# Two plain pairs at the head of each feed-forward layer, and a mixer input part in another order

## The chip, the core and the metric

The program runs on one core of a Trainium2 chip. The metric is device time in microseconds from launch to end, median of three runs. The engines are TensorE (PE in the profile, its weight loads PEld), VectorE (DVE), ScalarE (ACT), GpSimd (POOL) and SyncE (SP), which here issues the DMAs.

## The reference, cut to what matters

Two layers of a hybrid encoder trunk, over 576 tokens (512 of a new stream and 64 of a running one), with model width 1024 and feed-forward width 2816. Everything is float32.

```python
def swiglu_half(x, g, w_gate, w_up, w_down):
    h = rmsnorm(x, g)
    return x + 0.5 * ((jax.nn.silu(h @ w_gate) * (h @ w_up)) @ w_down)

def layer(x, ...):
    x = swiglu_half(x, ffn1...)
    y, c_kv, k_r, wkv, shift = token_mixer(rmsnorm(x, lp['mix_norm']), ...)
    x = x + y
    x = mem_attend(x, mk, mv, lp)
    x = swiglu_half(x, ffn2...)

def token_mixer(h, ...):
    proj = h @ lp['w_in']
    c_q, c_kv, k_r, p_b = jnp.split(proj, ...)     # latents of the attention heads; p_b feeds the recurrence
    ...                                            # 8 attention heads from c_q, c_kv, k_r
    xs = p_b + lp['shift_mu'] * (prev - p_b)
    r, k, v, xw, xa, xg = jnp.split(xs, ...)
    ...                                            # per-token recurrence over r, decay, k, v, kk, a
    y = y + jnp.sum(r_h * k_h * lp['r_k'], -1, keepdims=True) * v_h     # the "bonus"
    out = jnp.concatenate([y_a, y_b], axis=-1) @ lp['w_out']
```

## The kernel before, in words

**Matmuls.** Activations lie transposed, 128 features by 576 tokens to a tile, `x[0]` to `x[7]`. A float32 operand is cut into a high and a low part (`split`, L241 to L248: ACT writes the high part, another engine subtracts it from the source for the low one), and a product takes three matmuls (`mm3`, L312 to L316: high by high, high by low, low by high). The 576 tokens go as two halves `hs` of 288.

**Feed-forward layer** (`ffn`, four in the program). `Norm` (L362) takes the eight tiles one by one: high part, low part, square, and the squares are added into `nacc`, five of the seven additions on POOL (L378). Its `rstd` comes later, from a matmul with ones, and is applied to what comes out of PSUM. The width 2816 is 22 columns of 128, taken in 11 pairs. Pair 0 is plain: `plain` multiplies by a 1024 x 128 column, 48 matmuls, once for gate and once for up, for two columns. The other ten pairs go by a Strassen-Winograd scheme with 7 products in place of 8 (`products`): each needs 28 right-hand tiles `s`, made once per layer from the normed `x` (`normed`, `winograd`: four sums on POOL for every two tiles, and seven splits, two of whose low parts POOL makes), and per pair sums and splits of weight blocks (`factors`, 14 splits and 8 sums for gate and up). The gated activations of pair 0 are put into tiles with the tag `xnh`/`xnl`, of which there are eight each, all holding the normed input that `plain` reads. Down-projections follow: for pair 0 by themselves, then for every two pairs (`outputs`), each group of matmuls evicted by DVE onto `x` (L485, L594).

**Mixer input part** (`mixer`, L603 to L842). `STEPS` names the order: `key`, `gate`, `norms`, `factors`, `inverse` and `rest` for four groups of heads, and `keys`, `queries`, `rotated`, `normed` for the latents. `factors` multiplies on POOL at L722 and L724, `rest` at L773, and POOL also makes the low part of half of each streamed weight (`by=(DVE, POOL)`, L659). `rest` stores `rv` (L774), makes the bonus with the matmuls of L779 and stores it. The two last `rest` come after all latents. `inverse` runs a chain of 15 short products and reductions, the products on POOL for groups 0 and 1, on DVE for 2 and 3. All that the recurrence needs is stored to DRAM, and `prepare` (L1012) loads it back chunk by chunk (`ck`, `bk`, `DI`, L1015 to L1018).

**What sets the order.** A scheduler at build time walks the code with a model of each engine and fixes one in-order stream per engine. A tile that reuses a buffer waits until the former owner has been read for the last time. Each engine then runs its stream in order, SP its DMA issues too.

Of the kernel before, what the change touches and what calls it, by code (L numbers as in the profile page):

```python
# [10 lines left out]
F32R = mybir.dt.float32r  # L11
# [39 lines left out]
for _n, _c in (("ones", 128), ("eps", 4), ("id", 128), ("bd", 128), ("cen", 128), ("sel8", 32), ("sel", 128), ("mA", 256), ("mD", 64),  # L51
# [7 lines left out]
NT = 13  # L59
AHEAD = 4  # L60

# [3 lines left out]
         ("inverse", 1), ("factors", 3), ("inverse", 2), ("rest", 1), ("inverse", 3), ("keys",), ("queries",), ("rotated",),  # L65
         ("normed",), ("rest", 2), ("rest", 3))
# [65 lines left out]
def build(tc, I, O):  # L132
# [179 lines left out]
    def mm3(out, w, a, first, last, **kw):  # L312
        (wh, wl), (ah, al) = w, a
        PE.matmul(out, wh, ah, start=first, stop=False, **kw)  # L314
        PE.matmul(out, wh, al, start=False, stop=False, **kw)  # L315
        PE.matmul(out, wl, ah, start=False, stop=last, **kw)  # L316
# [45 lines left out]
    class Norm:  # L362
        def __init__(self, tiles, gain, tag, psum=None):
            self.out, self.tag = [], psum
            n = len(tiles)
            acc = st([128, T], "nacc")
            for k, t in enumerate(tiles):
# [4 lines left out]
                if k == 0:  # L372
                    ACT.activation(out=acc, in_=t, func=AF.Square)
                else:
                    s = st([128, T], "nsq")
                    ACT.activation(out=s, in_=t, func=AF.Square)  # L376
# [24 lines left out]
    def ffn(l, which, V, aside=iter(()), final=None, given=()):  # L401
# [3 lines left out]
        sc = Scope("ffn", side[1], s=28, sh=2, sl=2, sraw=1, S=4, t=NT)  # L405
# [18 lines left out]
        def winograd(b11, b12, b21, b22, alloc):  # L424

            t3, t1, t2, t4 = (tmp() for _ in range(4))
            for o, a, b, op in ((t3, b22, b12, ALU.subtract), (t1, b12, b11, ALU.subtract), (t2, t3, b11, ALU.add), (t4, b21, t2, ALU.subtract)):
                POOL.tensor_tensor(out=o, in0=a, in1=b, op=op)
            out = {}
            for n, src in ((1, b11), (6, t2), (7, t3), (5, t1), (2, b21), (4, t4), (3, b22)):  # L430
                t = out[n] = alloc()
                split(src, (t[:, 0], t[:, 1]), None, POOL if n in (5, 2) else DVE)
            return out

        def normed(j):
            y = []
            for k in (2 * j, 2 * j + 1):
                t = st([128, T], turn("nsq", "nacc"))
                DVE.scalar_tensor_tensor(out=t, in0=x[k], scalar=V("n%d" % which, k), in1=nrm.rstd(), op0=ALU.mult, op1=ALU.mult)
                y.append(t)  # L440
            return winograd(*[t[:, s] for t in y for s in hs], lambda: st([128, 2, HT], "s", F32R))


        ws = Stream(*[wgu[l, f, i] for f in range(2) for i in range(2)][len(given):] + [wd[l, g] for g in range(2)], given=given)
        xs, acts = [], []

        def plain(act):
            w, out = ws.next, []
            for s in hs:
                p = ps1("b")[:, 0:HT]  # L450
                for k in range(8):
                    mm3(p, w[k], [t[:, s] for t in act[k]], k == 0, k == 7)
                out.append((s, p))
            ws.ahead()
            return out

        for f in range(2):
            pg = plain(nrm.out)
            r = nrm.rstd()
            pu = plain(nrm.out)  # L460
            gs = []
            for s, p in pg:
                g = tmp()
                DVE.tensor_tensor(out=g, in0=p, in1=r[:, s], op=ALU.mult)
                silu(out=g, in_=g, func=AF.Silu)
                gs.append(g)
            acts.append((st([128, T], "xnh", F32R), st([128, T], "xnl", F32R)))
            for (s, p), g in zip(pu, gs):
                u = tmp()
                DVE.tensor_tensor(out=u, in0=p, in1=r[:, s], op=ALU.mult)  # L470
                DVE.tensor_tensor(out=u, in0=u, in1=g, op=ALU.mult)
                split(u, [t[:, s] for t in acts[f]], None)
            xs += [normed(2 * f), normed(2 * f + 1)]
        for i in range(2):
            w = ws.next
            pd = [[ps1("b")[:, 0:HT] for s in hs] for m in range(4)]
            for f in range(2):
                for m in range(4):
                    for s, p in zip(hs, pd[m]):
                        mm3(p, w[2 * m + f], [t[:, s] for t in acts[f]], f == 0, f == 1)  # L480
            ws.ahead()
            for m in range(4):
                for s, p in zip(hs, pd[m]):
                    o = x[4 * i + m][:, s]
                    DVE.scalar_tensor_tensor(out=o, in0=p, scalar=0.5, in1=o, op0=ALU.mult, op1=ALU.add)  # L485
# [3 lines left out]
        for p in range(1, NF // 2):  # L489
            order += [[wgu[l, 2 * q + r, i] for r in range(2)] for q, i in [(1, 0)] * (p == 1) + [(p, 1)] + [(p + 1, 0)] * (p + 1 < NF // 2)]  # L490
            if p % 2 == 0:
                order += [[wds[l, p // 2 - 1, m]] for m in range(4)]
# [92 lines left out]
        def outputs(ms, acts, halfway=None):  # L585
            ws = [take() for m in ms]
            for a in [hs[0:1], hs[1:2]] if halfway else [hs]:
# [7 lines left out]
                if halfway and a == hs[0:1]:  # L595
                    halfway()
# [902 lines left out]
```

## Time and profile before

| | us |
|---|---|
| three runs | 2869.1, 2871.0, 2876.91 |
| median | 2871.0 |
| the profiled execution, its own time | 2865.1 |
| its span, first to last instruction | 2863.2 |

The profiled execution is 5.9 us below the median. In the rows further down, columns are these. A row of a stretch gives for each engine its busy time and, in brackets, the number of instructions, then the mean granted clock of TensorE (1.00 is its full 2.4 GHz, 0.50 the lower level of 1.2 GHz). A row in order of time gives start and duration in us, engine, line, operation, the tile written and those read, and in square brackets the idle time before it with what ended it. Since matmuls overlap in the engine, the number of them that start in a stretch says more than their busy time.

### The profile page before, as it was taken

The page shows a single profiled execution, that of the slowest core. Times are in us where ns is not written, and L with a number is a line of the kernel's source. Part 1 is how long each engine was busy: PE and PEld are TensorE (multiplying, and loading weights), DVE is VectorE, ACT ScalarE, POOL GpSimd, SP SyncE. Part 2 cuts the span into 40 slices and gives each one's busy share as a digit, 9 for nine tenths or more (in the row PEclk, how much of TensorE's full clock was granted, in tenths as well). Part 3 has the DMA queues.
Part 4 walks back from the last instruction along what each step waited for, and adds up shares of the span by engine and source line. Part 5 has one row for each costly group of instructions (what it writes and reads, how often), then busy time and mean ns, then how long its engine had stood idle before and what let it go on. Part 6 is the DMA issues. An engine that isn't in the chain of part 4 may idle for free.

```text
span 2863.2 us, 56005 instructions
## 1 busy us (share of the span) xinstructions
PE 2753.5 (96%) x22188; PEld 2641.8 (92%) x22188; DVE 2129.2 (74%) x4216; ACT 1368.5 (48%) x2813; POOL 383.1 (13%) x461
## 2 busy tenths in 40 slices
PE   6999999889999989999989999998999999899998
PEld 6999999878889889999989999997888899899998
DVE  8887775866666678777787777768666765887776
ACT  5544455345554544444444444553555445444444
POOL 5000013610000030000040000245010001300000
PEclk8999999989999999999999999999999999999999
DMA  4333333652333122222212222346433332122221
GB/s 171 111 126 108 104 115 94 151 157 84 94 121 122 63 82 89 93 92 89 82 60 97 96 89 89 126 111 141 140 94 121 99 115 71 67 89 96 90 95 64
DMA packets 187576, 293.22 MB, mean 102 GB/s; under 512 B 87066, under 2 KB 113050, under 8 KB 187138
## 3 DMA queue, kind: packets, MB, share of 16 engines
q1 hardware_dynamic: 185010, 285.46, 31.9%
q0 software_dynamic: 2304, 4.20, 0.6%
q8 instruction: 174, 2.85, 0.4%
q14 instruction: 88, 0.72, 0.1%
HBM read 250.36 MB, written 41.63 MB: 102 GB/s over the span
## 4 chain that ended last, share of the span: by engine, by line
PE 89%; DVE 6%; ACT 1%; issue 1%; DMA 1%; POOL 0%; SPq 0%; DVEq 0%; ACTq 0%; POOLq 0%
PE b L314 18%; PE b L316 18%; PE b L315 18%; PE mm L314 4%; PE mm L315 3%; PE g L314 3%; PE mm L316 3%; PE g L315 3%; PE g L316 3%; PE sm L1001 2%; PE pp L1001 2%; PE sc L314 2%; PE pp L1025 1%; PE sc L316 1%; PE sc L315 1%
## 5 line engine op out<-in xcount | busy, mean ns | idle before, releaser
L246 ACT ACTIVATE whi<-wraw 128x512 fp32r<-128x512 f32 (+1 forms) x520 | 321.4, 623 | 483.5 <-PE b L315 221.4
L316 PE MATMUL b<-s,wlo 128*128 128x288 f32 x1536 | 450.4, 295 | 0.0
L315 PE MATMUL b<-s,whi 128*128 128x288 f32 x1536 | 449.0, 293 | 0.0
L314 PE MATMUL b<-s,whi 128*128 128x288 f32 x1536 | 448.1, 295 | 0.0
L247 DVE TENSOR_TENSOR wlo<-wraw,whi 128x512 fp32r<-128x512 f32 (+1 forms) x484 | 344.3, 715 | 113.2 <-ACT whi L246 94.1
L314 PE MATMUL b<-xnh,whi 128*128 128x288 f32 x1152 | 344.5, 308 | 38.0 <-ACT xnh L246 16.2
L315 PE MATMUL b<-xnl,whi 128*128 128x288 f32 x1152 | 349.5, 305 | 13.2 <-DVE xnl L247 9.3
L316 PE MATMUL b<-xnh,wlo 128*128 128x288 f32 x1152 | 345.9, 302 | 0.0
L315 PEld LDWEIGHTS b<-s,whi 128*128 128x128 f32 x1536 | 288.7, 188 | 0.0
L316 PEld LDWEIGHTS b<-s,wlo 128*128 128x128 f32 x1536 | 288.3, 188 | 0.0
L314 PEld LDWEIGHTS b<-s,whi 128*128 128x128 f32 x1536 | 286.8, 188 | 0.0
L314 PEld LDWEIGHTS b<-xnh,whi 128*128 128x128 f32 x1152 | 221.6, 196 | 44.6 <-ACT xnh L246 18.0
L378 POOL TENSOR_TENSOR nacc<-nacc,nsq 128x576 f32<-128x576 f32 x40 | 63.8, 1595 | 1399.6 <-ACT nsq L376 831.8
L594 DVE SCALAR_TENSOR_TENSOR x<-b,x 128x288 f32<-128x288 f32 x320 | 144.3, 455 | 140.7 <-PE b L316 140.4
L315 PEld LDWEIGHTS b<-xnl,whi 128*128 128x128 f32 x1152 | 225.4, 196 | 16.8 <-DVE xnl L247 11.3
L316 PEld LDWEIGHTS b<-xnh,wlo 128*128 128x128 f32 x1152 | 224.9, 196 | 0.1
L315 PE MATMUL b<-s,sh 128*128 128x288 f32 x704 | 208.7, 296 | 0.0
L314 PE MATMUL b<-s,sh 128*128 128x288 f32 x704 | 207.8, 295 | 0.0
L316 PE MATMUL b<-s,sl 128*128 128x288 f32 x704 | 207.8, 295 | 0.0
L246 ACT ACTIVATE whi<-S 128x512 fp32r<-128x512 f32 x188 | 118.0, 630 | 185.0 <-PE b L315 182.0
L314 PE MATMUL mm<-xnh,whi 128*128 128x288 f32 x688 | 205.1, 299 | 1.0 <-ACT xnh L370 1.0
L316 PE MATMUL mm<-xnh,wlo 128*128 128x288 f32 x688 | 203.6, 296 | 0.0
(455 smaller groups left out, 7517.3 us busy)
## 6 DMA issues: line engine op xcount, KB each, us to landing
wraw<-in_wgu SPq DMA_DIRECT2D x136, 512.0 KB
wraw<-in_wds SPq DMA_DIRECT2D x60, 512.0 KB
sraw<-in_wgu SPq DMA_DIRECT2D x40, 512.0 KB
wraw<-in_win SPq DMA_DIRECT2D x36, 512.0 KB
sraw<-in_wds SPq DMA_DIRECT2D x20, 512.0 KB
wraw<-in_wmk SPq DMA_DIRECT2D x16, 512.0 KB
wraw<-in_wmv SPq DMA_DIRECT2D x16, 512.0 KB
wraw<-in_wout SPq DMA_DIRECT2D x32, 256.0 KB
```

The source lines that it names most:

```text
L246: ACT.activation(out=h, in_=src, func=AF.Copy)
L247: by.tensor_tensor(out=lo, in0=src, in1=h.bitcast(F32), op=ALU.subtract)
L314: PE.matmul(out, wh, ah, start=first, stop=False, **kw)
L315: PE.matmul(out, wh, al, start=False, stop=False, **kw)
L316: PE.matmul(out, wl, ah, start=False, stop=last, **kw)
L378: e.tensor_tensor(out=acc, in0=acc, in1=s, op=ALU.add)
L594: DVE.scalar_tensor_tensor(out=o, in0=p, scalar=0.5, in1=o, op0=ALU.mult, op1=ALU.add)
L1001: PE.matmul(o, *f(p4, e), start=(n == 0 and p4 == 0), stop=(n == len(terms) - 1), skip_group_check=True)
L1025: PE.matmul(p[:, p4], bk[half(e), p4], ck[half(e), p4, 0:128], start=True, stop=True)
```

## The change

**Feed-forward.** `PLAIN = 2`: pairs 0 and 1 are plain (four columns), nine pairs go by the 7-product scheme. Plain weights come in half columns (`take(2)`), and `plain` runs both token halves over a half column before it goes on. The gated activations of the plain columns lie in `s`, `rr`, `a` and `rs` tiles. `right` makes the right-hand tiles of two `x` tiles after each plain column, wholly with DVE and ACT. The down-projection of pair 0 is put around the columns of pair 1, and that of pair 1 behind the first gate of pair 2. Pairs 2 to 9 are projected two by two, and pair 10 alone at the end. There are 9 `t` buffers for 13.

**Norm.** All squares come after the splits in the code, and all their sums are on DVE.

**Mixer.** L722, L724, L773 and the second weight half go from POOL to DVE. `rest` is cut into `rest` and `bonus`, the `rest` steps come before the latents, and the latents are last. The first chunk's products in `prepare` are ordered behind the first query matmuls (`after`).

```diff
-NT = 13
+NT = 9
+PLAIN = 2
-         ("inverse", 1), ("factors", 3), ("inverse", 2), ("rest", 1), ("inverse", 3), ("keys",), ("queries",), ("rotated",),
-         ("normed",), ("rest", 2), ("rest", 3))
+         ("inverse", 1), ("bonus", 0), ("factors", 3), ("inverse", 2), ("rest", 1), ("inverse", 3), ("rest", 2), ("bonus", 1),
+         ("rest", 3), ("bonus", 2), ("keys",), ("bonus", 3), ("queries",), ("rotated",), ("normed",))
...
-                    e = DVE if k in (6, 7) else POOL
-                    e.tensor_tensor(out=acc, in0=acc, in1=s, op=ALU.add)
+            acc = st([128, T], "nacc")
+            for k, t in enumerate(tiles):
+                s = st([128, T], "nsq") if k else acc
+                ACT.activation(out=s, in_=t, func=AF.Square)
+                if k:
+                    DVE.tensor_tensor(out=acc, in0=acc, in1=s, op=ALU.add)
...
-                POOL.tensor_tensor(out=o, in0=a, in1=b, op=op)
+                DVE.tensor_tensor(out=o, in0=a, in1=b, op=op)
-                split(src, (t[:, 0], t[:, 1]), None, POOL if n in (5, 2) else DVE)
+                split(src, (t[:, 0], t[:, 1]), None)
...
-            acts.append((st([128, T], "xnh", F32R), st([128, T], "xnl", F32R)))
+            act = [st([128, T], tag or turn("rr", "a", "rs"), F32R) for _ in range(2)]
...
+        for f in range(2 * PLAIN):
+            g = plain_gate()
+            if f == 3:
+                y = normed(f)
+            if f > 1:
+                all_outputs(acts[0:2], range(4 * f - 8, 4 * f - 4))
+            acts.append(plain_up(g, "s" if f < 2 else None))
+            xs.append(right(y if f == 3 else normed(f)))
+        g = gate()
+        all_outputs(acts[2:4])
+        acts = []
+        for p in pairs:
...
+            if (p - PLAIN) % 2:
+                all_outputs(acts)
+                acts = []
...
-        ws = Stream(*[win[l, j] for op in STEPS for j in columns(*op)], by=(DVE, POOL))
+        ws = Stream(*[win[l, j] for op in STEPS for j in columns(*op)])
-            POOL.tensor_tensor(out=kk, in0=kk, in1=av, op=ALU.mult)
+            DVE.tensor_tensor(out=kk, in0=kk, in1=av, op=ALU.mult)
-            POOL.tensor_tensor(out=xk, in0=xk, in1=av, op=ALU.mult)
+            DVE.tensor_tensor(out=xk, in0=xk, in1=av, op=ALU.mult)
-            POOL.tensor_tensor(out=rv[:, :, 0:64], in0=chunks(xr), in1=chunks(wts[p4]), op=ALU.mult)
+            DVE.tensor_tensor(out=rv[:, :, 0:64], in0=chunks(xr), in1=chunks(wts[p4]), op=ALU.mult)
...
+                    if c == order[0]:
+                        after(i, queried[0])
```

**Where instructions stand now.** VectorE in the second feed-forward layer of layer 0, before: `L471` ends the gated activation of the first plain column (`t`), and the row `xnl<-t,xnh` makes its low part.

```order
L471 TENSOR_TENSOR t<-t 128x288
L439 SCALAR_TENSOR_TENSOR nsq<-x,narrow,rstd 128x576
L247 TENSOR_TENSOR s<-t,s 128x288 x3
L247 TENSOR_TENSOR s<-nsq,s 128x288
L247 TENSOR_TENSOR s<-nacc,s 128x288
L247 TENSOR_TENSOR wlo<-wraw,whi 128x512
...
L464 TENSOR_TENSOR t<-b,rstd 128x288 x2
L247 TENSOR_TENSOR s<-t,s 128x288 x2
L470 TENSOR_TENSOR t<-b,rstd 128x288
L247 TENSOR_TENSOR s<-t,s 128x288
L247 TENSOR_TENSOR s<-nsq,s 128x288 x2
L247 TENSOR_TENSOR xnl<-t,xnh 128x288 x2
```

The same engine and layer in the changed kernel, at the third plain column: `L554` ends its gated activation and `a<-t,rr` makes the low part, in tiles of their own; `L501` are the sums that POOL made.

```order
L553 TENSOR_TENSOR t<-b,rstd 128x288 x2
L501 TENSOR_TENSOR t<-nacc,nsq 128x288
L501 TENSOR_TENSOR t<-nsq 128x288
L554 TENSOR_TENSOR t<-t 128x288
L248 TENSOR_TENSOR wlo<-wraw,whi 128x512
L554 TENSOR_TENSOR t<-t 128x288
L501 TENSOR_TENSOR t<-t,nsq 128x288
L248 TENSOR_TENSOR a<-t,rr 128x288
L501 TENSOR_TENSOR t<-nacc,t 128x288
L492 SCALAR_TENSOR_TENSOR nsq<-x,narrow,rstd 128x576
L248 TENSOR_TENSOR wlo<-wraw,whi 128x512
L248 TENSOR_TENSOR a<-t,rr 128x288
```

The activation's low part stands two to four rows behind its product instead of fourteen, and DVE has the sums in its own stream.

SyncE at the end of the mixer's input part in layer 0, before: the last `rest` stores `big` (L774), and the loads of the first chunk (`ck`, L1015) come three rows later. `d<-x` are the results of `inverse`, `d<-ad` the bonus.

```order
L766 DMA d_65<-x 36x16x16 x4
L256 DMA wraw<-in_wmv 128x1024
L842 DMA out_shift<-narrow 128x28
L766 DMA d_65<-x 36x16x16 x4
L774 DMA d_5259<-big 128x9x128
L782 DMA d_7068<-ad 128x576
L256 DMA wraw<-in_wmv 128x1024
L1015 DMA ck<-d_5259 128x768
L1016 DMA bk<-d_5260 128x512
L1018 DMA DI<-d_65 64x8x64 x2
```

SyncE at the same place in the changed kernel: the last `big` (L798), the bonus and two stores of latents (L846, L858), the loads of `ck` (L1043) and `bk`, and then the last results of `inverse` (L788), with the load of `DI` (L1046) behind them.

```order
L798 DMA d_5267<-big 128x9x128
L846 DMA out_ckv<-lx 128x576
L257 DMA wraw<-in_wmv 128x1024
L858 DMA out_krope<-lx 32x576
L810 DMA d_6919<-ad 128x576
L1043 DMA ck<-d_5267 128x768
...
L788 DMA d_65<-x 36x16x16 x4
L257 DMA wraw<-in_wmv 128x1024
L788 DMA d_65<-x 36x16x16 x4
L1046 DMA DI<-d_65 64x8x64 x4
```

Between the last store of `big` and the first load stands work of the latents; the last `inverse` is now what the first `DI` waits for.

## Rows read from the trace of the kernel before

**Rows 1.** The page, busy time, share of the span and instructions of each engine.
```profile
PE 2753.5 (96%) x22188; PEld 2641.8 (92%) x22188; DVE 2129.2 (74%) x4216; ACT 1368.5 (48%) x2813; POOL 383.1 (13%) x461
```
**Rows 2.** Busy time by stretch: starts of the four feed-forward layers, one steady stretch.
```profile
core 0: us, PE busy (x) PEld busy (x) DVE busy (x) ACT busy (x) POOL busy (x), PEclk, DMA share, GB/s
24.00:76.00 52.00, 40.67 (x243) 38.55 (x244) 47.97 (x81) 25.08 (x58) 29.02 (x24) 0.80 0.24 79
1036.00:1088.00 52.00, 41.16 (x261) 38.82 (x260) 47.82 (x80) 24.36 (x57) 25.64 (x24) 0.87 0.18 61
1444.00:1496.00 52.00, 42.97 (x283) 40.78 (x282) 49.14 (x85) 25.72 (x60) 27.39 (x24) 0.90 0.19 61
2448.00:2500.00 52.00, 43.88 (x278) 41.86 (x277) 48.50 (x84) 25.20 (x59) 27.29 (x24) 0.87 0.18 61
1100.00:1152.00 52.00, 52.00 (x395) 52.00 (x394) 44.67 (x87) 26.86 (x52) 0.00 (x0) 1.00 0.34 112
```
**Rows 3.** The same view of parts of the second start.
```profile
1030.60:1041.70 11.10, 10.62 (x77) 10.44 (x78) 5.38 (x11) 6.39 (x12) 0.00 (x0) 1.00 0.32 113
1057.70:1085.70 28.00, 17.16 (x84) 15.23 (x84) 27.36 (x50) 10.68 (x26) 13.14 (x13) 0.76 0.17 56
```
**Rows 4.** VectorE in order of time there: POOL silent at first, busy at the last row.
```profile
1041.69 0.82 DVE L464 TENSOR_TENSOR t<-b,rstd 128x288 f32<-128x288 f32 x2
1042.43 0.45 DVE L470 TENSOR_TENSOR t<-b,rstd 128x288 f32<-128x288 f32 x1
1042.79 1.54 DVE L439 SCALAR_TENSOR_TENSOR nsq<-x,narrow,rstd 128x576 f32<-128x576 f32 x2
1044.24 0.82 DVE L439 SCALAR_TENSOR_TENSOR nacc<-x,narrow,rstd 128x576 f32<-128x576 f32 x1
...
1045.34 0.69 DVE L247 TENSOR_TENSOR wlo<-wraw,whi 128x512 fp32r<-128x512 f32 x1
1045.94 0.46 DVE L247 TENSOR_TENSOR s<-nsq,s 128x288 fp32r<-128x288 f32 x1
...
1050.71 3.03 DVE L247 TENSOR_TENSOR s<-t,s 128x288 fp32r<-128x288 f32 x3
```
**Rows 5.** In order of time there, DVE, ACT and PE: the first activation tile.
```profile
1047.55 1.06 DVE L471 TENSOR_TENSOR t<-t 128x288 f32<-128x288 f32 x1
...
1058.60 0.76 ACT L246 ACTIVATE xnh<-t 128x288 fp32r<-128x288 f32 x2
...
1059.08 1.00 PE L314 MATMUL b<-xnh,whi 128*128 128x288 f32 x4 [1.36 <-ACT xnh L246]
```
**Rows 6.** Busy time by stretch: mixer input of layer 0 with its sum, sum of layer 1's.
```profile
538.00:558.00 20.00, 12.44 (x109) 10.47 (x108) 14.90 (x24) 7.53 (x12) 11.98 (x13) 0.83 0.79 173
...
578.00:598.00 20.00, 12.96 (x70) 10.81 (x68) 15.80 (x34) 10.07 (x21) 7.98 (x11) 0.82 0.69 175
598.00:614.00 16.00, 13.70 (x71) 12.98 (x72) 7.98 (x18) 6.55 (x14) 0.40 (x1) 0.69 0.68 166
sum 136.00, PE 118.18 PEld 107.25 DVE 104.96 ACT 55.02 POOL 68.20; mean PE 16.88 PEld 15.32 DVE 14.99 ACT 7.86 POOL 9.74
...
sum 130.00, PE 115.30 PEld 104.18 DVE 104.08 ACT 53.66 POOL 70.12; mean PE 16.47 PEld 14.88 DVE 14.87 ACT 7.67 POOL 10.02
```
**Rows 7.** The chain that ended last, between the last bonus and the recurrence: start, duration, what.
```profile
586.74 0.74 DVE xs L775
...
591.63 5.70 DMA d<-big
...
597.75 5.55 DMA bk<-d
603.34 1.16 PE pp L1025 x8
```
**Rows 8.** Lines by themselves, ns min/median/max; the last, of groups, busy us, mean ns.
```profile
L775 DVE SCALAR_TENSOR_TENSOR xs<-xs,narrow,xk x8: 801/806/3582, 502.0 to 2001.9; 128x576 f32<-128x576 f32 x8
L722 POOL TENSOR_TENSOR kk<-kk,x x8: 1416/1423/1942, 482.3 to 1952.4; 128x576 f32<-128x576 f32 x8
L247 POOL TENSOR_TENSOR wlo<-wraw,whi 128x512 fp32r<-128x512 f32 x36 | 48.3, 1341 | 53.0 <-ACT whi L246 53.0
```

More of the change, by code (lines that the diff above doesn't have):

```diff
@@ L315, in mm3 @@
         PE.matmul(out, wh, al, start=False, stop=False, **kw)
-        PE.matmul(out, wl, ah, start=False, stop=last, **kw)
+        return PE.matmul(out, wl, ah, start=False, stop=last, **kw)
     def mmT(p, w, act, first, last):
@@ L435, in normed @@
[L435 to L466, printed above, removed]
-            acts.append((st([128, T], "xnh", F32R), st([128, T], "xnl", F32R)))
[L468 to L485, printed above, removed]
@@ L494, in factors @@
+        order += [[wd[l, PLAIN, g]] for g in range(2)]
         def factors():
-            for aps in order:
+            for n, aps in enumerate(order):
+                if n < len(given):
+                    yield from given[n].parts
+                    continue
                 blocks = []
@@ L529, in ffn, with take @@
         made, ready = factors(), []
-        def take():
-            while len(ready) <= AHEAD:
+        def take(ahead=None):
+            while len(ready) <= (AHEAD if ahead is None else ahead):
                 hl = next(made, None)
@@ new lines, in outputs @@
+        def outputs(acts, ms, halfway=None):
+            n = len(acts)
+            per = 4 // n
+            ws = [take() for _ in range(len(ms) // per)]
+            for a in [hs[0:1], hs[1:2]] if halfway else [hs]:
+                for i, m in enumerate(ms):
+                    for s in a:
+                        p = ps1("b")[:, 0:HT]
+                        for f in range(n):
+                            mm3(p, cols(ws[i // per], i % per * n + f), [t[:, s] for t in acts[f]], f == 0, f == n - 1)
+                        o = x[m][:, s]
+                        DVE.scalar_tensor_tensor(out=o, in0=p, scalar=0.5, in1=o, op0=ALU.mult, op1=ALU.add)
+                if halfway and a == hs[0:1]:
+                    halfway()
@@ new lines, in all_outputs, with plain @@
+        def all_outputs(acts, ms=range(8)):
+            per = 4 // len(acts)
+            for m in ms[::per]:
+                outputs(acts, range(m, m + per))
+        def plain(act):
+            ps = [ps1("b")[:, 0:HT] for _ in hs]
+            for i in range(2):
+                w = take(2)
+                for s, p in zip(hs, ps):
+                    for k in range(4):
+                        mm3(p, cols(w, k), [t[:, s] for t in act[4 * i + k]], i + k == 0, i * k == 3)
+            return list(zip(hs, ps))
@@ L547, in products @@
                 for n in range(4):
[L548 removed]
+                    mm3(bank[at], cols(w, n), [bs[n][i][:, e] for e in range(2)], at == i and n == 0, n == 3, skip_group_check=True)
                 yield i, bank[at]
@@ L806, in mixer @@
         SP.dma_start(gD, xg)
-        at = {"key": key, "gate": gate, "norms": key_norms, "factors": factors, "inverse": inverse, "rest": rest}
+        at = {"key": key, "gate": gate, "norms": key_norms, "factors": factors, "inverse": inverse, "rest": rest, "bonus": bonus}
         for op, *n in STEPS:
```

114 lines of the change are left out of this document (64 added, 50 removed).

## Prediction

> **What bounds the kernel now.** I read the page's busy line first [rows 1]: TensorE is busy for 96% of the span, VectorE for 74%. So the time can only fall where TensorE is short of work, and the next view, busy time by stretch, is for finding those places. The steady stretch starts 395 matmuls in 52 us, 0.1316 us each [rows 2]. The heads of the four feed-forward layers start 243, 261, 283 and 278: 152 + 134 + 112 + 117 = 515 too few, or 515 x 0.1316 = 67.8 us. The reader should see that VectorE is busy there for about 48 of 52 us (0.92), and that the granted clock falls below 1.00 after TensorE has gone idle. In 28 us of the second head 84 matmuls start where 213 would fit, at clock 0.76 [rows 3].
>
> The rows in order of time say what TensorE waits for. The gated product was made at 1047.55, but its high part only starts at 1058.60, and the matmul that follows the tile's split comes at 1059.08 [rows 5]: 11 us lie between, since the split writes into a tile that the plain matmuls still read. After that VectorE, which makes the right-hand tiles, is itself late. Part of its lateness is length: while POOL is silent a 288-wide operation takes 0.37 us from start to start, a 576-wide one 0.73 and a 512-wide one 0.60; beside POOL's sums three 288-wide ones took 3.03, about 1.0 each [rows 4].
>
> In the mixer input part TensorE is idle for 136 - 118.2 = 17.8 us in layer 0 and 130 - 115.3 = 14.7 in layer 1 [rows 6]. In three stretches of layer 0 the clock was 0.83, 0.82 and 0.69, which is 6.8 + 7.2 + 9.9 = 23.9 us at the lower level, worth at most half, 12 us. The chain of waits tells the end of it: the last bonus product, a store of 5.70 us, a load of 5.55 us, and the recurrence's first matmul at 603.34, 16.6 us after the bonus [rows 7].
>
> **Plain pairs: added matmuls.** A pair by 7 products takes 168 matmuls for gate and up, a plain one 192. That is 24 more in each of four layers: 96 x 0.1316 = **+12.6 us**.
>
> **Plain pairs: the head's stall.** In the new order each activation has tiles that nobody reads at that time, so its low part stands right behind the product, and the 11 us wait goes. What is late next? TensorE now has 384 plain matmuls, 96 of projections and 12 of the first right-hand product before it needs the second product's tile, and 77 of these start before `rstd` arrives at 1041.7 [rows 3]. The other 415 last 415 x 0.1316 = 54.6 us. VectorE's stream has between the same points 89 operations of 288, 8 of 576 and 23 of 512: 89 x 0.37 + 8 x 0.73 + 23 x 0.60 = 52.6 us at the paces of [rows 4], or 57 at its 0.92 share. So it comes about 2.6 us late by the end, and is hardly ahead anywhere. I keep **4 us** of stall in each layer, **+16**, against the 17 that each loses now. The bounds are 0 (VectorE without gaps, 52.6 under 54.6) and 9 (half of today's loss). POOL's work hidden there is zero after the change: its 16 sums and 8 low parts in each layer have gone into the 89. The half-column weights move the same bytes, at a DMA share of about 0.2 [rows 2], and cost nothing. Nine `t` buffers: the most held at once are seven; if they ran out, VectorE would wait as it now does on the activation tile, which is the last rival.
>
> **Feed-forward ends.** With pair 10 alone, each output needs the newest activation. From its last product that is a VectorE sum and product (2 x 0.37), a high part on ACT (two took 0.76 [rows 5], so 0.38) and a low part (0.37): 1.5 us, nothing else queued for TensorE. Four times makes **+6**. The bounds: 0 if the memory or mixer weights' matmuls fill it, 4 each if VectorE's evictions (16 x 0.37 beside 8 x 0.73 of the next norm's low parts) are late.
>
> **Norm sums.** Five of 0.73 us go from POOL to VectorE in each of eight norms. I take nothing: the first 77 matmuls of a head run while `rstd` is made, at full pace [rows 3], and the sums replace POOL's in that shadow. Without that cover it is 5 x 0.73 = 3.7 us a norm; the range holds that for a few of them.
>
> **Mixer input part.** VectorE takes over 12 products of 576 (12 x 0.73 = 8.8 us) and 12 weight low parts in this stretch (12 x 0.60 = 7.2; the other six lie ahead of it): +16 us. POOL's own durations for these are 1.42 and 1.34 us [rows 8], some 33 us gone from POOL. What does that give back to VectorE? Its `xs` step took 3582 ns once, beside a median of 806 [rows 8]. Bounds: nothing, or 33 us times VectorE's busy share of 105/136, 25 us. I take 10, below the middle, because the median is close to the uncontended 0.73. VectorE then needs 105 + 16 - 10 = 111 us, at a share of 0.92 121 of the 136 us; in layer 1 104 + 16 - 10 = 110, or 120 of 130.
>
> TensorE's side: with the stores first, the 5.70 and 5.55 us transfers lie beside the latents. What is late next is the latents' own chain into the first query, behind which the first chunk's products are now ordered, with the whole recurrence queued after them. It isn't shown before; bounds 0 and the 16.6 us of the chain that it replaces [rows 7], I take half, 8. SyncE passes the last `inverse` stores late, and the loads of `DI` queue behind; a store and a load of that kind are within the same 16.6. So TensorE needs 118.2 - 12 + 8 = 114. The larger of 121 and 114 binds in layer 0 (gain 15), 120 in layer 1 (gain 10): **-25**. Bounds: a loss of 50 (below), and a gain of 17.8 + 12 + 14.7 + 12 = 56 if all idleness and slow clock goes.
>
> **The sum.** The profiled execution took 2865.1 us. 2865.1 - 67.8 + 16 + 12.6 + 6 - 25 = 2806.9. It lies 5.9 below the median of the runs, 2871.0, so the forecast for the median is 2806.9 + 5.9 = **2813 us**. A change within 0.3% (8.6 us) cannot be told from none.
>
> **Rivals.** *VectorE binds the mixers.* If nothing comes back from POOL's silence, 121/0.92 = 132 of 136 and 120/0.92 = 130 of 130: no gain there worth counting. 2806.9 + 25 + 5.9 = 2838. For it: the median of 806, which leaves little to return. Against it: the one step of 3582 [rows 8], on the kind of operation that the last chain starts from [rows 7].
>
> *POOL's silence gives everything back.* VectorE's long operations vanish, heads need 52.6 us under a cover of 54.6 (no stall), and the mixers' VectorE needs 105 + 16 - 25 = 96, at its 0.92 share 104 us, so TensorE binds, with 114 of 136 and 115.3 - 12 + 8 = 111 of 130: gains of 22 and 19 in place of 15 and 10. 2806.9 - 16 - 16 + 5.9 = 2781. For it: 1.0 against 0.37 [rows 4]. Against it: the median 806 [rows 8]. The Trainium skill (SBUF — State Buffer, "Who interferes with whom") says that a VectorE instruction with two SBUF inputs and a GpSimd one that reads SBUF contend, and describes the contested port pair as an exclusive lock. By that rule each microsecond of POOL's reading costs VectorE up to the same, the side of this rival; the 3582 ns agree with it for one instruction, the median does not show it for the rest.
>
> *VectorE only gets more work* (the slower side). The long operations are then the stage's own and not POOL's doing. If a quarter of the 89 in each head still take 1.0 us, their mean is 0.53 and VectorE needs 89 x 0.53 + 5.8 + 13.8 = 66.8 us, 12 more than the cover (48 in place of 16); in the mixers 105 + 19 = 124 at today's share of 0.77 need 161 for 136, 25 more in each layer. 2865.1 - 67.8 + 48 + 12.6 + 6 + 50 + 5.9 = 2920. It decides from the point where VectorE's mean 576-wide two-input operation stays above 0.9 us with POOL silent. Against it: the rows in which POOL is silent hold 0.37 and 0.73 at the same tiles [rows 4]. The Trainium skill (Perfetto Trace Analysis, "Optimizing Scalar/DVE Operations") advises the reverse of this change: where VectorE is saturated, work may go to other engines, even GpSimd, though the two share a port and it might not help. VectorE at 0.92 in the heads is the case that the advice means; by it alone the 48 and 50 of this rival would stand.
>
> *The change doesn't remove the wait.* The new activation tiles or the nine `t` still have readers when the split wants them, about 12 us stay in each head, and the mixers gain nothing: 2865.1 - 67.8 + 48 + 12.6 + 6 + 5.9 = 2870, no change.
>
> **How the numbers follow.** Chances: the forecast 0.58, with a range of its own of 2787 to 2834 (its stall terms at 0 or 7 us a layer, the mixers at 10 either way); VectorE binding the mixers 0.17; everything given back 0.14; VectorE with only more work 0.06; the wait stays 0.05. The range for 8 in 10 leaves out the last two and the outer parts of the second and third, some 0.2 together: from 2774 to 2850. Faster by over 0.3% are the first three, 0.89; within 0.3% the wait that stays, 0.05; slower, with VectorE's extra work, 0.06.
>
> **What would show it.** Heads: 350 or more matmuls in those 52 us stretches at clock 1.00, and no wait of TensorE on an activation tile; 288-wide low parts at 0.37 us beside the sums. If the stall stays, the row of `a<-t` or the `s` low part that TensorE waits for names the engine. Ends: 1 to 2 us of idle TensorE before the first output of pair 10. Mixers: VectorE's busy share near 0.9 and no idle TensorE before a load of `bk`; in its place a wait on the latents' norm, or on `DI`. No `xs` step near 3.6 us. I would be wrong if VectorE's 576-wide operations stayed above 0.9 us, if the heads waited on weights instead, or if the recurrence's start moved later by more than the 16.6 us that it has now.

## The result, and the profile after

| | before | changed kernel |
|---|---|---|
| median, us | 2870.05 | 2836.54 |
| lowest to highest of four runs, us | 2865.87 to 2876.91 | 2832.89 to 2839.47 |
| the profiled execution, us | 2865.1 | 2836.0 |
| its span, us | 2863.2 | 2834.2 |

The ratio is 0.9884, with a 95% interval of 0.9866 to 0.9903. The kernel became 33.5 us faster where 58 were forecast; 2836.5 lies in the range of 2774 to 2850.

The page's busy line, which answers [rows 1]:

```profile
PE 2745.4 (97%) x22284; PEld 2634.1 (93%) x22284; DVE 2116.6 (75%) x4412; ACT 1351.2 (48%) x2781; POOL 136.2 (5%) x265
```

POOL has lost 196 instructions and 247 us. VectorE has 196 instructions more and yet is busy 12.6 us less. So its instructions have become shorter, as the forecast supposed: in the second head three 288-wide low parts take 1.19 us together in order of time, where they took 3.03 [rows 4]:

```profile
1041.13 1.19 DVE L248 TENSOR_TENSOR s<-t,s 128x288 fp32r<-128x288 f32 x3
```

The heads of the four feed-forward layers by stretch, which answer [rows 2]:

```profile
24.00:76.00 52.00, 52.00 (x395) 52.00 (x394) 48.83 (x113) 25.08 (x57) 0.00 (x0) 1.00 0.29 97
1026.00:1078.00 52.00, 52.00 (x392) 51.79 (x391) 46.35 (x105) 26.11 (x59) 0.00 (x0) 1.00 0.23 75
1424.00:1476.00 52.00, 50.35 (x364) 49.79 (x365) 45.91 (x103) 25.60 (x59) 0.00 (x0) 0.97 0.21 72
2429.00:2481.00 52.00, 52.00 (x391) 51.79 (x390) 46.35 (x105) 26.10 (x59) 0.00 (x0) 1.00 0.23 76
```

Where 243 to 283 matmuls started, 364 to 395 do, with the clock at 1.00 in three of the four. The third stretch begins while TensorE still waits for the norm sums of the layer end before it (1.8 us). The waits of TensorE from 1010 to 1100 us hold a single line, and it is a weight, not an activation tile:

```profile
PE b L315 <- ACT whi L247: 0.6, 1, 0.6
```

The end of the first feed-forward layer by stretch (same columns; the window begins 22.6 us before the layer's last matmul in both kernels), before:

```profile
404.00:456.00 52.00, 51.74 (x386) 51.06 (x385) 33.45 (x50) 31.68 (x52) 18.23 (x20) 1.00 0.38 128
```

and after:

```profile
388.00:440.00 52.00, 47.67 (x342) 45.59 (x342) 42.75 (x74) 33.68 (x57) 3.16 (x10) 1.00 0.39 136
```

Here 44 fewer matmuls start. The chain of waits at this place, after, gives start, duration, engine, tile and line:

```profile
409.48 1.23 DVE big L248
410.70 0.37 DVE x L521
411.07 0.72 DVE xnl L371
411.80 0.37 DVE x L521
412.17 0.67 DVE nacc L378
412.83 0.60 DVE wlo L248
...
419.99 0.77 DVE nacc L378
...
420.80 1.24 PE g L386 x4
```

From 409.5 to 420.8 the path runs on VectorE almost without a break: evictions onto `x`, low parts, norm sums, low parts of weights. TensorE waits for VectorE here. The forecast had put 1.5 us here, for the newest activation of the lone pair; the waits for that activation are 0.6 and 0.7 us, and those for `nacc`, `xnl` and `x`, 1.4, 0.9 and 0.3 us, come on top.

The end of the mixer's input part in layer 0 by stretch, with the sum of 462 to 598, which answers [rows 6]:

```profile
542.00:562.00 20.00, 17.35 (x124) 15.52 (x122) 14.44 (x41) 7.56 (x14) 3.03 (x6) 1.00 0.79 216
562.00:582.00 20.00, 8.26 (x31) 6.42 (x29) 19.69 (x59) 11.47 (x21) 8.11 (x9) 0.59 0.62 169
582.00:598.00 16.00, 14.04 (x82) 12.67 (x82) 9.27 (x21) 7.02 (x16) 0.53 (x1) 0.76 0.53 124
sum 136.00, PE 119.65 PEld 108.78 DVE 106.37 ACT 57.14 POOL 41.09; mean PE 17.09 PEld 15.54 DVE 15.20 ACT 8.16 POOL 5.87
```

The idle time of TensorE, 17.8 us before, is 16.4 us now, and VectorE is busy for 106.4 us where it was 105. The two earlier idle places have become one. In 562 to 582 VectorE is full (19.69 of 20) and only 31 matmuls start. The longest wait from 536 to 600 us:

```profile
PE g L315 <- DVE vpl L248: 9.9, 1, 9.9
```

and the chain of waits there, which answers [rows 7]:

```profile
564.90 0.40 DVE x L783 x2
565.30 0.31 DVE x L784 x2
...
571.05 1.45 DVE lx L868 x2
572.71 0.67 DVE qnl L248
573.53 0.72 DVE qnl L248
...
575.02 0.60 DVE x L783
575.62 0.60 DVE vpl L248
...
588.86 1.08 PE pp L1053 x8
```

The store of 5.70 us and the load of 5.55 us [rows 7] have left this chain. In their place stand the latents' steps (`rs`, `rr`, `lx`, `qnl`, `vpl`) in VectorE's stream, with links of the two `inverse` chains that run on VectorE (L783, L784) between them. In the order of before, the matmuls of the last `rest` follow the latents; these now come earlier, the recurrence is held behind the queries, and nothing is left for TensorE. It works again from 576.4 on, but from there to 586.4 the same view gives a mean clock of 0.51, and 0.76 from 582 to 598.

For a balance over the whole program I took from each matmul's start-to-start time its share at full pace (0.1316 us for 288 columns, fewer columns in proportion, at least 0.055 us) and summed what was above it by stage. Four stages moved:

| TensorE's lost time, us | before | after | difference | forecast |
|---|---|---|---|---|
| four heads | 79.8 | 14.2 | -65.6 | -51.8 |
| ends of the four layers, and the next 52 us | 15.7 | 32.5 | +16.8 | +6 |
| rest of the two mixer input parts | 70.4 | 65.3 | -5.1 | -25 |
| recurrence with attention, two layers | 138.7 | 152.0 | +13.3 | 0 |
| 96 more matmuls x 0.1316 | | | +12.6 | +12.6 |

The five rows make -28.0; the profiled executions differ by 29.1. The recurrence is counted from its first product to the memory layer's first matmul: 286.2 us before and 290.5 after in layer 0, 283.8 and 290.7 in layer 1. The gain that the forecast missed was lost at the ends, in the mixers and in the recurrence behind them. The heads even did better than forecast.

### The profile page after: what moved, and what is told of

Same layout as the page of the kernel before. It is cut to its first block, busy times and chain, and to the rows that moved or that the text cites. A ratio compares the mean times of both kernels' runs of the same rounds, so it can differ in the third digit from the quotient of the medians.

```text
span 2834.2 us, 56032 instructions
## 1 busy us (share of the span) xinstructions
PE 2745.4 (97%) x22284; PEld 2634.1 (93%) x22284; DVE 2116.6 (75%) x4412; ACT 1351.2 (48%) x2781; POOL 136.2 (5%) x265
## 4 chain that ended last, share of the span: by engine, by line
PE 91%; DVE 5%; ACT 2%; DMA 1%; issue 1%; SPq 0%; DVEq 0%; POOL 0%; ACTq 0%
PE b L315 18%; PE b L316 18%; PE b L317 18%; PE mm L315 4%; PE mm L316 4%; PE mm L317 4%; PE g L315 3%; PE g L316 3%; PE g L317 3%; PE sm L1029 2%; PE sc L315 2%; PE pp L1029 2%; PE sc L317 1%; PE sc L316 1%; PE pp L1053 1%; PE tp L982 1%
## 5 line engine op out<-in xcount | busy, mean ns | idle before, releaser
L247 ACT ACTIVATE whi<-wraw 128x512 fp32r<-128x512 f32 (+1 forms) x493 | 305.7, 623 | 545.0 <-PE b L316 264.6
L248 DVE TENSOR_TENSOR wlo<-wraw,whi 128x512 fp32r<-128x512 f32 (+1 forms) x493 | 333.8, 680 | 111.5 <-ACT whi L247 94.1
L317 PE MATMUL b<-s,wlo 128*128 128x288 f32 x1388 | 407.4, 295 | 0.0
L316 PE MATMUL b<-s,whi 128*128 128x288 f32 x1388 | 406.0, 293 | 0.0
L315 PE MATMUL b<-s,whi 128*128 128x288 f32 x1388 | 404.9, 295 | 0.0
L521 DVE SCALAR_TENSOR_TENSOR x<-b,x 128x288 f32<-128x288 f32 x448 | 197.0, 456 | 132.9 <-PE b L317 132.5
L316 PEld LDWEIGHTS b<-s,whi 128*128 128x128 f32 x1388 | 260.7, 188 | 0.0
L317 PEld LDWEIGHTS b<-s,wlo 128*128 128x128 f32 x1388 | 260.6, 188 | 0.0
L315 PEld LDWEIGHTS b<-s,whi 128*128 128x128 f32 x1388 | 258.9, 188 | 0.0
L316 PE MATMUL b<-s,sh 128*128 128x288 f32 x756 | 223.8, 296 | 0.0
L317 PE MATMUL b<-s,sl 128*128 128x288 f32 x756 | 222.8, 295 | 0.0
L315 PE MATMUL b<-s,sh 128*128 128x288 f32 x756 | 222.7, 295 | 0.0
L316 PE MATMUL mm<-xnl,whi 128*128 128x288 f32 x688 | 204.5, 297 | 1.1 <-DVE xnl L371 0.9
```

Source lines behind the costliest of these rows:

```text
L247: ACT.activation(out=h, in_=src, func=AF.Copy)
L248: by.tensor_tensor(out=lo, in0=src, in1=h.bitcast(F32), op=ALU.subtract)
L317: return PE.matmul(out, wl, ah, start=False, stop=last, **kw)
```

## The experiments

**Heads: the tile, POOL, or the cover?** Three things changed there at once: the activation got tiles of its own, the sums went from POOL to VectorE, and a second plain pair lies over the work. First the tiles alone, in the kernel before (with nine `t` buffers for thirteen, as in the changed kernel):

```diff
-NT = 13
+NT = 9
...
-        sc = Scope("ffn", side[1], s=28, sh=2, sl=2, sraw=1, S=4, t=NT)
+        sc = Scope("ffn", side[1], s=28, sh=2, sl=2, sraw=1, S=4, t=NT, a=2)
...
-            acts.append((st([128, T], "xnh", F32R), st([128, T], "xnl", F32R)))
+            acts.append([st([128, T], n, F32R) for n in (("rr", "a"), ("a", "rs"))[f]])
```

Expected:

> The kernel of before with the gated activations of pair 0 in tiles of their own (rr, two of a, rs) and nine t buffers for thirteen; one plain pair and all POOL work stay. If the tile that the plain matmuls still read was the main wait, some 11 us come back in each head, 44 in all: about 2829. If VectorE and POOL are late with the right-hand tiles in any case, with one plain pair as the only cover, 0 to 4 us come back in each: 2857 to 2873.

Measured: 2875.1 us, ratio 1.0019 [1.0007, 1.0031]. Nothing came back. By stretch the first two heads are as before, and in the third and fourth 262 and 259 matmuls start, where it was 283 and 278:

```profile
24.00:76.00 52.00, 39.97 (x243) 37.23 (x244) 46.01 (x81) 24.91 (x58) 28.81 (x24) 0.84 0.24 84
1036.00:1088.00 52.00, 40.95 (x259) 38.79 (x258) 47.35 (x77) 23.83 (x56) 27.38 (x24) 0.80 0.17 55
```

The tile's delay is gone: the first high part starts at 1046.05, where it was 1058.60 [rows 5]. But TensorE had lost little by it, the 1.36 us in brackets in [rows 5]. Its waits on activation tiles from 1030 to 1110 us, before:

```profile
PE b L314 <- ACT xnh L246: 4.7, 2, 3.4
PE b L315 <- DVE xnl L247: 2.7, 2, 1.7
```

and with tiles of their own:

```profile
PE b L314 <- ACT a L246: 4.8, 2, 2.5
PE b L315 <- DVE rs L247: 2.6, 1, 2.6
```

They are now all for the second column. Its gated products (L471) come at 1066.84 and 1075.72, before at 1065.88 and 1074.24, and VectorE has no idle gap from 1040.8 to 1082.5. So VectorE's backlog stood behind the tile, as late as ever; a want of `t` buffers does not show. Then the same with the sums and low parts on VectorE, still one plain pair:

```diff
-                POOL.tensor_tensor(out=o, in0=a, in1=b, op=op)
+                DVE.tensor_tensor(out=o, in0=a, in1=b, op=op)
...
-                split(src, (t[:, 0], t[:, 1]), None, POOL if n in (5, 2) else DVE)
+                split(src, (t[:, 0], t[:, 1]), None)
```

> The kernel of before with activation tiles of their own (nine t buffers) and the sums and low parts of the right-hand tiles on VectorE in place of POOL; still one plain pair. Theory that the second plain pair is what matters, as cover: with one pair 192 + 96 + 12 - 77 = 223 matmuls, 29 us, lie over some 40 us of VectorE's work, so 10 us a layer stay lost and the time is 2850 to 2870. Rival, POOL (its sums that VectorE waits for, and the stretched operations) is the cause: the heads lose under 3 us each, 2815 to 2830.

Measured: 2850.6 us, 0.9932 [0.9918, 0.9947], at the low end of the theory's range.

```profile
24.00:76.00 52.00, 44.44 (x292) 43.35 (x292) 47.28 (x110) 27.22 (x62) 0.00 (x0) 0.87 0.26 86
1036.00:1088.00 52.00, 46.34 (x313) 44.63 (x312) 51.58 (x115) 24.88 (x59) 0.00 (x0) 0.90 0.17 54
```

From 259 to 313 matmuls in the second head, with VectorE at 51.58 of 52 us. So about 25 us come from POOL's silence as long as the cover is short, and VectorE's own work then binds. The converse puts POOL back under the two plain pairs of the changed kernel:

```diff
-                DVE.tensor_tensor(out=o, in0=a, in1=b, op=op)
+                POOL.tensor_tensor(out=o, in0=a, in1=b, op=op)
...
-                split(src, (t[:, 0], t[:, 1]), None)
+                split(src, (t[:, 0], t[:, 1]), None, POOL if n in (5, 2) else DVE)
```

> The changed kernel with the four sums and two of the seven low parts of each right-hand set on POOL again, in all four feed-forward heads; the activation tiles stay the new ones. If POOL beside VectorE stretches the 288-wide operations to about 1.0 us as in the trace of before, VectorE falls behind TensorE in the heads and 4 to 10 us a layer are lost: 2853 to 2877. Rival, the activation tile's wait was all of the old stall: POOL takes work off VectorE and costs nothing, 2832 to 2840.

Measured: 2837.5 us, 0.9892 [0.9877, 0.9907], the same as the changed kernel. Two rows of VectorE in order of time:

```profile
1055.36 2.04 DVE L248 TENSOR_TENSOR s<-nsq,s 128x288 fp32r<-128x288 f32 x2
1057.33 0.45 DVE L544 TENSOR_TENSOR t<-b,rstd 128x288 f32<-128x288 f32 x1
```

POOL at that time, in the same view:

```profile
1056.07 1.02 POOL L501 TENSOR_TENSOR t<-nacc,nsq 128x288 f32<-128x288 f32 x1
1057.05 1.03 POOL L501 TENSOR_TENSOR t<-nsq 128x288 f32<-128x288 f32 x1
```

And the second head by stretch:

```profile
1036.00:1088.00 52.00, 52.00 (x393) 51.85 (x392) 48.79 (x87) 22.59 (x53) 24.29 (x22) 1.00 0.21 72
```

Beside POOL two low parts with both inputs in SBUF take 2.04 us, while a product that reads PSUM (`t<-b,rstd`) takes 0.45 as ever. The stretched operations are there, and 393 matmuls start all the same (376 in the first head). With 415 matmuls over VectorE's work either placement is nearly in time, with one pair neither is, so the cover is what counts. No run has the second plain pair without what came with it, the half columns and the moved down-projection, so the cover is theirs together.

The Trainium skill (SBUF — State Buffer, "Who interferes with whom") tells the two rows apart by the number of SBUF inputs, and these rows agree. What it costs in time is another matter: 25 us with the short cover, nothing that can be seen with the long one.

**Ends: the moved norm sums, or the lone pair?** Two edits load VectorE there. The sums back on POOL:

```diff
-                    DVE.tensor_tensor(out=acc, in0=acc, in1=s, op=ALU.add)
+                    (DVE if k in (6, 7) else POOL).tensor_tensor(out=acc, in0=acc, in1=s, op=ALU.add)
```

> The changed kernel with five of the seven sums of each norm on POOL again. Theory that the moved sums make VectorE late at the ends of the feed-forward layers (17 us lost there more than before): some 8 us come back, about 2828. Rival, the lone last pair alone makes VectorE late with its evictions: no gain, and POOL beside VectorE stretches it, 2836 to 2842.

Measured: 2837.6 us, 0.9888 [0.9868, 0.9908]. No gain: at the first end 344 matmuls start in the 52 us.

```profile
392.00:444.00 52.00, 47.90 (x344) 45.84 (x344) 42.85 (x69) 33.88 (x57) 11.93 (x15) 1.00 0.39 137
```

But VectorE was not relieved. It has 69 instructions for 74 and is busy as long, 42.85 us for 42.75: beside POOL's sums, 1.4 to 1.9 us each, its 576-wide low parts take up to 1.62 us, and 0.82 in the changed kernel. So this run doesn't show what the sums cost where nothing contends.

Then the lone pair at the front of the nine and the others two by two up to the end (with the weights packed to suit):

```diff
-            if (p - PLAIN) % 2:
+            if (p - PLAIN) % 2 == 0 and not end:
                 all_outputs(acts)
                 acts = []
...
-            if (p - PLAIN) % 2:
-                order += [[wds[l, (p - PLAIN) // 2, m]] for m in range(4)]
-        order += [[wd[l, PLAIN, g]] for g in range(2)]
+            if p == PLAIN:
+                order += [[wd[l, PLAIN, g]] for g in range(2)]
+            elif (p - PLAIN) % 2 == 0:
+                order += [[wds[l, (p - PLAIN) // 2 - 1, m]] for m in range(4)]
```

> The changed kernel with the lone product pair projected first (pair 2) and the others two by two up to the end, so that an output at the end has 12 matmuls behind it and not 6. Theory that the lone pair at the end makes VectorE late: lost time at the ends falls from 17 us more than before to about 5, total about 2825. Rival, the moved norm sums make it late in any case: at most 4 us come back, 2832 to 2838.

Measured: 2809.8 us, 0.9786 [0.9765, 0.9806], 27 us faster than the changed kernel, more than either theory gave. The same window:

```profile
388.00:440.00 52.00, 51.73 (x385) 51.06 (x384) 37.09 (x60) 31.99 (x52) 2.00 (x6) 1.00 0.37 128
```

385 matmuls start in place of 342. By the balance the ends give about 17 us and the mixers with the recurrence about 9. The working that the forecast should have made: a tile of `x` is two outputs. With a lone pair these have 2 x 6 matmuls, 1.58 us, in which VectorE owes two evictions (2 x 0.37), a low part (0.73) and a sum (0.67), 2.14 us; with two pairs the two outputs have 24 matmuls, 3.16 us. The one order leaves VectorE behind at each tile, the other leaves it time for the weights too. The sums stay on VectorE here, so the place of the lone pair is enough to explain the loss at the ends; without its sum a tile would need 1.47 us under 1.58, which no run tries without POOL.

**Mixer: the engines, the steps, or the order behind the queries?** First the whole mixer of before under the changed feed-forward layers: the steps of before, its three products and the second weight halves on POOL, no order behind the queries.

```diff
...
-        ws = Stream(*[win[l, j] for op in STEPS for j in columns(*op)])
+        ws = Stream(*[win[l, j] for op in STEPS for j in columns(*op)], by=(DVE, POOL))
...
-            DVE.tensor_tensor(out=kk, in0=kk, in1=av, op=ALU.mult)
+            POOL.tensor_tensor(out=kk, in0=kk, in1=av, op=ALU.mult)
...
-                    if c == order[0]:
-                        after(i, queried[0])
```

> The changed feed-forward layers and norms with the mixer of before: its order of steps, its POOL products and weight low parts, no order between first queries and recurrence. Theory from the two traces: TensorE's lost time from the mixer's start to the end of the recurrence was 36.2 + 34.2 before the recurrence and 70.6 + 68.1 in it, and is 33.4 + 31.9 and 75.9 + 76.1 in the changed kernel, so the mixer edits cost 8 us and this gives about 2828. The forecast's own term (mixer edits gain 25) would give about 2861.

Measured: 2837.3 us, 0.9884 [0.9863, 0.9904]. The mixer edits together are worth nothing, neither the forecast's 25 nor the loss of 8 that I read from the two traces. That kernel's order with the changed kernel's engines (no product and no low part of a weight on POOL):

```diff
-         ("inverse", 1), ("bonus", 0), ("factors", 3), ("inverse", 2), ("rest", 1), ("inverse", 3), ("rest", 2), ("bonus", 1),
-         ("rest", 3), ("bonus", 2), ("keys",), ("bonus", 3), ("queries",), ("rotated",), ("normed",))
+         ("inverse", 1), ("factors", 3), ("inverse", 2), ("rest", 1), ("inverse", 3), ("keys",), ("queries",), ("rotated",),
+         ("normed",), ("rest", 2), ("rest", 3))
...
             held[p4] = xr, vt
+            if ("bonus", p4) not in STEPS:
+                bonus(p4)
...
-                    if c == order[0]:
-                        after(i, queried[0])
```

> The changed kernel with the mixer's steps in the order of before (and no order between first queries and recurrence), its products and weight low parts staying on VectorE. With the feed-forward part alone (2837) it differs in the engines only, with the changed kernel (2837) in the order only. Theory that VectorE is what limits the mixer's input part: VectorE with more work in the old order loses some 8 us a layer there, about 2850. Rival, POOL's work was neither hidden nor dear: within 5 us of 2837. Third, the order is what costs and the engine change gains: 2825 or less.

Measured: 2826.4 us, 0.9853 [0.9836, 0.9871]. Against the kernel above only the engines differ. The 11 us are what taking products and low parts from POOL gives, if they are real: the intervals just overlap, and the two profiled spans differ by 6 (2830.6 and 2824.6). By the balance 65.3 us are lost in the input parts for 75.4, and 8 more in the recurrence. So the changed kernel's order loses what its engines gain. The changed kernel without its one line of order:

```diff
                     i = PE.matmul(p[:, p4], bk[half(e), p4], ck[half(e), p4, 0:128], start=True, stop=True)
-                    if c == order[0]:
-                        after(i, queried[0])
```

> The changed kernel without the order that puts the first chunk's products behind the first query matmuls. If that order delays the recurrence (the forecast kept 8 us a layer for the latents' chain), the first recurrence product starts earlier and 5 us or more come back, 2825 to 2832. Rival, what the first chunk waits for is its own load, which comes as late: within 4 us of 2837.

Measured: 2826.1 us, 0.9850 [0.9832, 0.9867]: 10 us come back with one line, and the steps are then worth nothing beside the 2826.4. The recurrence's first product starts at 573.7 in place of 588.9, and the longest waits of TensorE from 536 to 600 us are

```profile
PE pp L1053 <- DMA bk<-d: 4.0, 1, 4.0
PE pp L1029 <- DMA DI<-d: 2.6, 2, 1.7
```

The load's wait of [rows 7] is back, but shorter than the 9.9 us for which the queries held the recurrence; the wait on `vpl` itself is down to 1.5.

A second suspect for those 9.9 us were the `inverse` chains themselves, which can run on POOL:

```diff
-        IV = (POOL, POOL, DVE, DVE)
+        IV = (POOL, POOL, POOL, POOL)
```

> The changed kernel with the products of all four inverse chains on POOL, so that two of them leave VectorE's stream at the end of the mixer's input part. Theory that these chains hold up the latents there (TensorE waits 9.9 us on a low part that stands behind them in layer 0): the wait falls under 4 us, the recurrence starts 6 to 8 us earlier in each layer, about 2822. Rival, the chains on POOL end later and the load of their result becomes the last wait before the recurrence: no gain or slower, 2836 to 2850.

Measured: 2831.0 us, 0.9860 [0.9841, 0.9878], 5.5 us less, with intervals that overlap. The mechanism did not go as expected, since the wait only fell to

```profile
PE g L315 <- DVE vpl L248: 8.7, 1, 8.7
```

The chain of waits there holds, after the latents' sums at 563.6 (`mm`), the steps of their own norm, on ACT and then on VectorE:

```profile
566.36 0.69 ACT rs L300
567.08 0.77 DVE rs L349
...
568.66 1.69 DVE lx L868 x2
...
572.78 0.61 DVE vpl L248
```

Only the short reductions of the `inverse` chains (L784) are left on VectorE between them, with waits of 0.24 and 0.30 us for POOL's products, and 8.7 of 9.9 us remain. So the wait is for the most part the latents' own chain, the one that the forecast names, and not the `inverse` chains.

**Together.** Three kernels put the lone pair first, as above, with one or two mixer edits beside it. All `inverse` products on POOL (`IV`):

> The changed kernel with the lone pair projected first and all inverse chains on POOL. If the two gains (27 and 5.5 us) lie at different places they add: about 2805. If the second is only the schedule's luck in the recurrence: 2808 to 2814.

Measured: 2809.0 us, 0.9791 [0.9774, 0.9809], no gain over the lone pair alone (2809.8).

The line `after(i, queried[0])` left out:

> The changed kernel with the lone pair projected first and without the order behind the first query matmuls, in its own order of the mixer's steps. The kernel with the old steps and the lone pair first took 2796 and has no such order either. If that order is the whole loss and the steps themselves are worth nothing, 2793 to 2800. If the new steps are worth something by themselves, below 2790 or above 2803.

Measured: 2814.9 us, 0.9811 [0.9797, 0.9825]. That is above 2803, the side on which the steps matter by themselves. Leaving the line out, 10 us faster with the lone pair last, now gives nothing: 5 us slower, with intervals that overlap.

That line left out, and the steps of before:

> The changed kernel with the lone pair projected first and the mixer's steps in the order of before, all products on VectorE. The two edits alone gave 27 and 10 us. If they lie at different places they add: about 2800. If the 10 us of the old order came from what the end of the feed-forward layer left to the mixer's start, little is left of it: 2806 to 2812.

Measured: 2796.2 us, 0.9744 [0.9727, 0.9761], the best of all: 40 us faster than the changed kernel and 74 faster than before. Neither this kernel nor the one of 2814.9 has the line, and both have the same engines; only the steps differ, and those of before are 18.7 us faster. With the lone pair last the same two orders were 0.3 us apart (2826.4 and 2826.1). Stretches from the mixer's start to the recurrence, and from there to the memory layer, with their sum, for this kernel:

```profile
412.90:582.60 169.70, 158.85 (x1170) 146.27 (x1168) 128.09 (x272) 88.32 (x149) 45.88 (x81) 0.96 0.53 137
582.60:864.00 281.40, 275.55 (x3005) 245.73 (x3005) 188.69 (x470) 151.75 (x382) 18.29 (x43) 1.00 0.37 110
```

and for the changed kernel:

```profile
411.20:588.80 177.60, 159.32 (x1167) 145.49 (x1167) 131.89 (x277) 88.16 (x149) 46.82 (x82) 0.94 0.52 139
588.80:879.30 290.50, 283.57 (x3007) 251.08 (x3006) 191.39 (x473) 153.82 (x385) 17.53 (x42) 0.99 0.34 104
```

The same recurrence takes 281.4 us or 290.5. In the kernel of 2814.9 it starts earlier and is longer:

```profile
565.40:869.90 304.50, 292.01 (x3049) 260.31 (x3050) 203.73 (x506) 163.75 (x404) 24.38 (x51) 0.96 0.35 107
```

Both stretches together take 451.1, 468.1 and 459.2 us. Of the 23.1 us between 304.5 and 281.4, 44 more matmuls, which have moved into this stretch, are some 5.8 at 0.1316 each, and the clock of 0.96 for 1.00 is at most 0.04 x 304.5 = 12. Between 290.5 and 281.4 the clock is at most some 3 us. The rest is in how the scheduler interleaves attention and recurrence, and no run here takes that apart. The mixer edits do not add, and what sets the length of the recurrence under them is not settled.

## Why the forecast was right in direction and short in size

- **Plain pairs, added matmuls:** +12.6, as worked out.
- **Plain pairs, the head's stall:** right that it goes, and too careful: 4 us a layer were kept, and by the balance 1.3 to 2.8 are left in each of the last three. VectorE's list of 52.6 us fits under the 54.6 us of cover, as the rival with everything returned had it. The reading that the activation tile was the first cause fell: own tiles alone give nothing, and of the 11 us between product and matmul TensorE was idle on that tile for 1.36.
- **POOL beside VectorE:** the stretching is as read [rows 4], about 1.0 against 0.37, and the longest `xs` step is 0.82 us where it was 3.58. Its worth depends on the cover, 25 us or nothing. One reading of [rows 4] was wrong: POOL is not silent in the rows of 1045.34 and 1045.94. It has two sums there, which took 3.82 us, and VectorE's rows kept their pace.
- **Feed-forward ends:** mis-sized, +6 against +16.8, outside its bounds in two of the layers. What it priced is there, 1.3 us for 1.5 at the first end. VectorE's backlog was left for the bound, and there as 16 x 0.37 + 8 x 0.73 = 11.8 us, which fits under the lone pair's 96 matmuls (12.6 us); with the seven norm sums of 0.67, costed at nothing, it is 16.5. The place of the lone pair decided it; what the sums add by themselves is not shown.
- **Mixer input part:** -25 forecast, 0 measured. The engines' share is a gain of 11 at best. The step that failed is "TensorE needs 118.2 - 12 + 8 = 114". The 8 for the latents' chain was close: TensorE waits 9.9 us on it in layer 0 and 10.4 in layer 1. The 12 for the clock did not come back. By the forecast's own working, 24.1 us of the stretch are at the lower level now (0.59 and 0.76 above), 23.9 before, and TensorE's idle time went from 17.8 to 16.4. One wait replaced another, with the clock falling behind it as before. VectorE's total did not bind either: it came to 106.4 us of 136 and is full only where TensorE waits. The line that orders the first chunk behind the queries costs 10 us in all, and the lost time in the recurrence grew by 13.3, for which I had no term.
- **Luck:** the heads gave 13.8 us more than forecast, while ends, mixers and recurrence together fell short by 44. Without the heads' surplus the time would have been some 2850, the upper end of the range.
- **The rivals:** the time of "VectorE binds the mixers", 2838, is the measured one, but not by its mechanism. POOL's silence seems to return time there, and the order takes it. That VectorE only gets more work is excluded by its busy time, which fell. The wait of TensorE on an activation tile is gone, so the change does what it says.

## What to carry to other kernels

When a tile comes late, look at how long its reader sat idle, and at what else is late there. An activation's split stood 11 us behind its product, TensorE idled 1.36 us before it, and freeing the tile alone gave nothing; twice the independent matmuls over the same work gave nearly everything. Put the shortest group of matmuls where the engine that drains it has nothing else to do, not at a layer's end, where the next layer's norm wants the same engine: here work per output tile (2.14 us) against cover (1.58 or 3.16) told it, and moving the lone pair gave 27 us. An order written by hand to keep one chain early can hold back a longer one, and its worth may change with the next edit, so measure such lines again after every other change.

## What the runs showed of the hardware

A VectorE operation with both inputs in SBUF took about 1.0 us from start to start beside POOL's sums, where its pace alone is 0.37; one with an input in PSUM kept 0.36 while POOL's sum went on. It is not always VectorE that pays. In the trace of before, POOL's two sums

```profile
1044.48 3.82 POOL L428 TENSOR_TENSOR t<-nsq 128x288 f32<-128x288 f32 x2 [23.33 <-DVE nsq L439]
```

took 1.9 us each, where later ones took 1.02, while the VectorE rows beside them kept 0.60 and 0.37 [rows 4]. Times on POOL are the roughest of the trace, so this is a hint and not a proof.

After TensorE had been idle from 566.4 to 576.4, its mean granted clock was 0.51 in the 10 us in which it worked again, and 0.85 from 586.4 to 598. So an idle place is paid for again in the busy time that follows.
